# Two LayerNorms of an encoder block: three of eight quarter turnings go by DMA, one weight tile's low half moves, and the matmuls behind them go by pairs of K tiles

## The chip, the cores and the metric

One core of a Trainium2 chip runs the whole program. The metric is the device time in microseconds (us) of one execution; several executions of each kernel are timed and their median is given. Engines: TensorE (PE; PEld is its weight load), VectorE (DVE), ScalarE (ACT), GpSimd (POOL) and SyncE (SP, whose queue issues most DMAs).

## The reference

One encoder layer on 256 tokens of width 2048, all in float32, weights read once from HBM:

```python
h = x
h = LN(alpha*h + 0.5*SwiGLU_1(h))          # ln_ffn1
h = LN(alpha*h + hybrid_mixer(h))          # ln_mix
h = LN(alpha*h + CrossAttn(h, LN(mem)))    # ln_x
h = LN(alpha*h + 0.5*SwiGLU_2(h))          # ln_ffn2
# hybrid_mixer: proj = u @ w_in, split into q, k, v of a chunked attention,
# two latents, and two gates; then both attentions, gating and w_out
def layer_norm(x, g, b):
    mu = x.mean(-1); var = square(x - mu).mean(-1)
    return (x - mu) * rsqrt(var + eps) * g + b
```

## The kernel before

**Tiling.** The 256 tokens are two token tiles (tt 0 and 1) of 128. The width of 2048 is 16 K tiles of 128, kept as four blocks T0 to T3 of four K tiles each: the normalised activations turned, features on partitions, as a high and a low half. The residual stream stays as h0 and h1, one tile of 128x2048 for each token tile (`h0_101`, `h1_102` in the order; without numbers `h_101`, `h_102`).

**Matmuls.** A float32 product is made of three passes over halves: high x high, high x low, low x high. Of each weight tile (1 MB, `raw`, read by the SP queue at L193, three buffers in turn) ACT rounds two pieces of 1024 columns to the high half (`halves`, L264), and DVE subtracts to make the low half (L267). High and low halves of a tile lie in two buffers in turn, or, where a tag names a home, in blocks such as H5/H0 or X0/X1 that stay until both token tiles have used them. A weight tile is 128x2048: four K tiles of 512 columns, or a pair of K tiles of 2 x 512 columns.

**A LayerNorm after a projection.** `ln_scale` takes mean and scale from the statistics: an aggregation (L395) and eight small steps (L400 to L403) on DVE. `ln_T` then does one quarter (q) after the other, 512 columns each, eight quarters for both token tiles: normalise h on DVE (even q) or on ACT (odd q), four PE transposes of 128x128 into a PSUM tile `at` (L421), gain and bias on the way out, two on ACT (L428) and two on DVE (L430), and `split`: a rounding on ACT (L255) and the low half on DVE (L256), both into T0 (q = 0) to T3 (q = 3).

**A LayerNorm that turns by DMA.** The one in the middle, ln_mix, uses `turned_norm`: ACT copies a normalised quarter into two planes of 16-bit words (`planes`, L846), the SP queue sends a DMA transpose of 128x1024 words (`send`, L850), ACT joins the two planes again (`join`, L854), and gain and bias (L1426 on ACT, L1428 on DVE) and the split follow.

**The stretch behind ln_ffn1 and ln_x.** Four weight tiles are used twice, first with token tile 0, then with token tile 1 (`skewed`), so that PE has work on tile 0 while tile 1 is still being normalised. After ffn1 these are the value weights w_va (`val` in `mixer`): one column half n = 0 with four K tiles for each weight tile, 48 matmuls for tile 0, 48 for tile 1; then column half n = 1 with both tiles, 96 matmuls. After the cross attention, `first_group` does the same with the first gate columns of ffn2 and then its first up columns. Behind them come w_gate groups and ffn2 groups, which go by `pair_group` and `mm_pair`: a pair of K tiles, two column groups and both token tiles, four PSUM tiles at once, and form sums of activations and of weights for some pairs (`Sums`, `forms_step`).

**Order.** The program is written as a list of steps with the weight tiles they need (`add`); `weave` puts side steps, the LayerNorm's among them, between main steps, and `run` emits weight loads and halves some tiles ahead. The tile framework keeps each engine's order by this list and by priorities; `issue_after` puts an instruction behind another in the order without a semaphore of its own. Each queue, SP's too, goes in its order: an instruction that waits holds what is behind it. A load in `fetch` stands behind the last transpose sent (`self.sent`), and `send` stands behind the last load.

## Time and profile before

| what | us |
|---|---|
| median of 3 executions | 2433.03 (2432.76 to 2437.99) |
| the profiled execution | 2432.52 |
| its span on the core | 2430.7 |
| PE busy in the span | 2422.3 |
| DVE busy | 2130.9 |
| ACT busy | 1553.2 |
| matmuls and transposes on PE | 11280 instructions |

How to read it: the span runs from the first to the last instruction of one profiled execution; its own time lies 1.8 us above it. "Busy" of PE is modelled, and a matmul that stands and waits for its operand can count as busy, so small waits show only when times between two rows are held against the number of matmuls between them. The chain of waits follows the last instruction back to what released it; where it names PE, PE was the engine on which the end depended.

### The profile page before, as it was taken

To read this page: it belongs to the slowest core of one execution; us is meant where nothing else is said; L and a number is where in the kernel's file an instruction comes from. 1 tells how busy PE (TensorE), PEld (TensorE's weight loads), DVE (VectorE), ACT (ScalarE), POOL (GpSimd) and SP (SyncE) were. 2 spreads that over 40 slices of the span, in tenths; PEclk is the share of its full clock that TensorE was granted. 3 is DMA by queue.
4 is the path that set the end of the run, shared out by engine and by line. 5 is a ranking of instruction groups with operands and counts; after the bars stand their busy time and mean duration, and the time that the engine had idled before them with its cause. 6 is when DMAs were issued, how large, how long until landed. Compare 5 with 4: busy or idle time off the path is not lost.

```text
span 2430.7 us, 29702 instructions
## 1 busy us (share of the span) xinstructions
PE 2422.3 (100%) x11280; PEld 2022.8 (83%) x11280; DVE 2130.9 (88%) x2437; ACT 1553.2 (64%) x2022; POOL 35.9 (1%) x81
## 2 busy tenths in 40 slices
PE   9999999999999999999999999999999999999999
PEld 8888888888888888888888888888888888888887
DVE  8999989899889998779788889979879999888997
ACT  6676745666555557878565687765666675556662
POOL 0000000000000001000000000000000000000000
PEclk9999999999999999999999999999999999999999
DMA  7766656667656657776577577655556766666665
GB/s 268 252 212 214 207 200 222 210 201 219 224 176 215 216 195 248 229 210 176 183 246 256 167 241 213 220 181 192 190 199 214 229 221 210 220 207 207 200 220 182
DMA packets 176414, 516.20 MB, mean 212 GB/s; under 512 B 111728, under 2 KB 112496, under 8 KB 121104
## 3 DMA queue, kind: packets, MB, share of 16 engines
q1 hardware_dynamic: 170816, 495.83, 61.6%
q0 software_dynamic: 4592, 17.30, 2.2%
q8 instruction: 88, 1.44, 0.2%
q10 hardware_dynamic: 864, 1.18, 0.1%
q14 instruction: 54, 0.44, 0.1%
HBM read 485.30 MB, written 2.10 MB: 201 GB/s over the span
## 4 chain that ended last, share of the span: by engine, by line
PE 89%; DVE 4%; ACT 3%; DMA 1%; issue 1%; SPq 0%; DVEq 0%; ACTq 0%
PE at L311 24%; PE mm L311 23%; PE at L366 11%; PE mm L366 11%; PE mm L298 10%; PE mm L277 4%; PE mm L279 2%; DVE lo L267 2%; ACT hi L264 1%; PE at L1034 1%; PE at L1505 0%; PE at L277 0%; DMA raw<-w_xv 0%; PE at L1088 0%; ACT H L854 0%
## 5 line engine op out<-in xcount | busy, mean ns | idle before, releaser
L264 ACT CAST hi<-raw 128x1024 fp32r<-128x1024 f32 (+1 forms) x852 | 804.0, 981 | 458.0 <-PE at L311 150.1
L267 DVE TENSOR_TENSOR lo<-raw,hi 128x2048 fp32r<-128x2048 f32 (+1 forms) x427 | 902.0, 2114 | 134.8 <-ACT hi L264 129.0
L311 PE MATMUL mm<-hi,T 128*128 128x512 f32 (+1 forms) x1312 | 307.5, 384 | 0.8 <-DVE v L400 0.7
L311 PEld LDWEIGHTS mm<-hi,T 128*128 128x128 f32 x1312 | 244.5, 188 | 46.9 <-DVE v L400 1.1
L264 ACT CAST X<-H 128x1024 fp32r<-128x1024 f32 (+1 forms) x170 | 174.8, 1035 | 160.9 <-DVE H L248 119.9
L311 PE MATMUL at<-hi,T 128*128 128x512 f32 x1136 | 272.3, 390 | 0.0
L311 PEld LDWEIGHTS at<-hi,T 128*128 128x128 f32 x1136 | 213.3, 188 | 44.5
L267 DVE TENSOR_TENSOR X<-H,X 128x2048 fp32r<-128x2048 f32 (+1 forms) x85 | 191.4, 2252 | 64.7 <-ACT X L264 64.7
L311 PE MATMUL mm<-lo,T 128*128 128x512 f32 (+1 forms) x656 | 158.4, 383 | 0.0
L311 PE MATMUL at<-lo,T 128*128 128x512 f32 x568 | 141.0, 389 | 0.0
L311 PEld LDWEIGHTS mm<-lo,T 128*128 128x128 f32 x656 | 122.3, 188 | 22.4
L311 PE MATMUL at<-hi,H 128*128 128x512 f32 x560 | 133.8, 390 | 0.0
L311 PEld LDWEIGHTS at<-lo,T 128*128 128x128 f32 x568 | 106.7, 188 | 22.1
L311 PEld LDWEIGHTS at<-hi,H 128*128 128x128 f32 x560 | 105.0, 188 | 21.5
L250 DVE TENSOR_TENSOR H<-H,raw 128x512 f32<-128x512 f32 (+1 forms) x170 | 115.4, 679 | 2.2
L311 PE MATMUL mm<-hi,H 128*128 128x512 f32 x480 | 115.5, 392 | 0.1
L311 PEld LDWEIGHTS mm<-hi,H 128*128 128x128 f32 x480 | 89.6, 188 | 18.9 <-DVE w L684 0.5
L248 DVE TENSOR_TENSOR H<-raw 128x1024 f32<-128x1024 f32 (+1 forms) x85 | 102.1, 1201 | 0.6 <-DMA raw<-w_gate 0.4
L366 PE MATMUL mm<-X,X 128*128 128x512 f32 x342 | 91.4, 393 | 0.0
L264 ACT CAST X<-raw 128x1024 fp32r<-128x1024 f32 (+1 forms) x54 | 55.4, 1035 | 47.9 <-DVE raw L250 38.6
L366 PE MATMUL at<-X,X 128*128 128x512 f32 (+1 forms) x315 | 82.6, 386 | 0.7 <-ACT X L264 0.7
L854 ACT COPY w<-w 128x1024 uint16<-128x1024 uint16 (+1 forms) x60 | 75.7, 1275 | 1.4 <-DMA w<-w 1.4
(387 smaller groups left out, 4151.3 us busy)
## 6 DMA issues: line engine op xcount, KB each, us to landing
raw<-ffn_w_in SPq DMA_DIRECT2D x150, 1024.0 KB, 4.9
raw<-ffn_w_out SPq DMA_DIRECT2D x66, 1024.0 KB, 4.9
raw<-w_gate SPq DMA_DIRECT2D x32, 1024.0 KB, 4.8
raw<-ffn_w_out_r SPq DMA_DIRECT2D x16, 1024.0 KB, 4.9
raw<-w_qk SPq DMA_DIRECT2D x16, 1024.0 KB, 5.6
raw<-w_o_b SPq DMA_DIRECT2D x16, 1024.0 KB, 4.8
raw<-w_out SPq DMA_DIRECT2D x16, 1024.0 KB, 5.0
raw<-w_xk SPq DMA_DIRECT2D x16, 1024.0 KB, 5.4
```

Source lines behind the costliest of these rows:

```text
L248: self.nc.vector.tensor_tensor(two[0], two[1], raw[:, :m].unsqueeze(1).to_broadcast([P, 2, m]), ALU.add)
L250: self.nc.vector.tensor_tensor(t[:, a * m:a * m + m], t[:, b * m:b * m + m], raw[:, a * m:a * m + m], ALU.add)
L264: self.last_hi = self.nc.scalar.copy(hi[:, c:d], src[:, c:d])
L267: self.last_lo = self.nc.vector.tensor_tensor(lo[:, :n], src, hi[:, :n].bitcast(F32), ALU.subtract)
L277: self.nc.tensor.matmul(ps, hi[j], x.both(kt), start=(j == 0), stop=False)
L279: self.last_mm = self.nc.tensor.matmul(ps[:, :S], lo[j], x.at(0, kt), start=False, stop=(j == n - 1))
L298: self.last_mm = self.nc.tensor.matmul(ps, x.at(xi, kt)[:, tt * P:(tt + 1) * P], w[wi][:, j * 512 + c:j * 512 + c + m], start=(start and j ...
L311: self.last_mm = self.nc.tensor.matmul(ps[tt, g][:, :n], x.at(xi, kt)[:, tt * P:(tt + 1) * P], w[wi][:, c:c + n], start=first and j + wi + ...
L366: self.last_mm = self.nc.tensor.matmul(bank[:, :m], a[xi], v[wi][:, c * m:(c + 1) * m], start=own and first and wi + xi == 0, stop=own and ...
L854: self.nc.scalar.copy(self.words(u, n).rearrange("p (c k) -> p k c", k=2), self.words(s, n).rearrange("p (k c) -> p k c", k=2))
L1034: nc.tensor.matmul(ps[:, c0:c0 + nk], q[:, tt * P:(tt + 1) * P], k[:, :nk], start=(j == 0), stop=(j == len(parts) - 1))
```

## The change

It touches the LayerNorm behind ffn1 and the one behind the cross attention in the same way, and the stretch of matmuls behind each.

- Of eight quarters three go by planes, DMA transpose and join: q = 2 and q = 3 of token tile 0 and q = 3 of token tile 1. The planes and joined data lie in the blocks F and X2. Five quarters stay on PE: 20 transposes instead of 32.
- The low half of the third weight tile (H0 after ffn1, X1 after the cross attention; tag "after") is put behind the last low half of token tile 0's quarters, where it stood ahead of them.
- The planes are put behind the rounding of T1, the transposes between weight loads, the joins behind roundings of weight tiles.
- The weights are packed by pairs of K tiles, and `skewed_pairs` takes the place of `val` and of `first_group`'s own steps: token tile 0 with K tiles 0 to 7 and both column groups (48 matmuls), token tile 1 with the same (48), then K tiles 8 to 15 with both token tiles (96). The value copies come after all of these. The form sums move from between the second column half's steps to steps 9 and on.
- Two groups behind, w_gate and w_lat, take the other of two PSUM banks.

```diff
@@ run(), load() @@
         for i in range(len(main) + 1):
             for f in side.get(i, ()):
-                self.add(f, prio=prio, held=main[i][2] if i < len(main) else 0)
+                f, p = f if isinstance(f, tuple) else (f, prio)
+                self.add(f, prio=p, held=main[i][2] if i < len(main) else 0)
...
                 with self.tc.issue_after(first.ins) if first else nullcontext():
-                    got = self.halves(raw[:, :ap.shape[1]], hi, lo)
+                    got = self.halves(raw[:, :ap.shape[1]], hi, lo, bool(tags) and "after" in tags)
@@ split(), halves() @@
-        self.nc.vector.tensor_tensor(lo, src, hi.bitcast(F32), ALU.subtract)
+        self.last_split = self.nc.vector.tensor_tensor(lo, src, hi.bitcast(F32), ALU.subtract)
         return copied
-    def halves(self, src, hi, lo):
+    def halves(self, src, hi, lo, late=False):
...
-        with self.tc.issue_after(self.chain.ins) if self.chain is not None else nullcontext():
-            self.last_lo = self.nc.vector.tensor_tensor(lo[:, :n], src, hi[:, :n].bitcast(F32), ALU.subtract)
+        def low(behind=None):
+            first = behind or self.chain
+            with self.tc.issue_after(first.ins) if first is not None else nullcontext():
+                self.last_lo = self.nc.vector.tensor_tensor(lo[:, :n], src, hi[:, :n].bitcast(F32), ALU.subtract)
+        if late:
+            self.late.append(low)
+        else:
+            low()
@@ ln_T() @@
             turned = self.split(v, hi, lo)
-            if q == 1:
-                self.ln_act = turned
+            if q == qs[-1]:
+                self.ln_act, self.ln_lo = turned, self.last_split
+        while self.late:
+            self.late.pop(0)(self.ln_lo)
@@ first_group() @@
-        first = self.collect(lambda: self.skewed(
-            part, (), (None, None, ("X0", "X1", "early"), ("H4", "H5"))))
-        self.weave(first, dict(zip((0, 3, 4), before)))
...
+        side = dict(before)
+        for i, c in enumerate(SUMS_IN):
+            side.setdefault(9 + i, []).append((self.forms_step(fx, SUMS_IN, c, xT), 0))
+        self.skewed_pairs(self.t[tag + "_w_in"][0], ps, xT, side, (None, None, ("X0", "X1", "early", "after"), ("H4", "H5")))
@@ new @@
+    def skewed_pairs(self, src, ps, xT, side, tags):
+        kept = {}
+        def add(k, tts, tags=None, held=0, keep=False, again=False):
+            def fn(w=None):
+                if keep:
+                    kept[k] = w
+                w = kept.pop(k) if again else w
+                if k == 0:
+                    ps.update({(tt, g): self.group_tile(0) for tt in tts for g in range(2)})
+                self.mm_pair(ps, w, 512, xT(), (2 * k, 2 * k + 1), k == 0, k == 7, tts)
+            self.add(fn, *(() if again else ((src[:, k * 2048:(k + 1) * 2048], tags),)), held=held)
+        def build():
+            self.skewed(lambda tt, k, **kw: add(k, (tt,), **kw), (), tags)
+            for k in range(4, 8):
+                add(k, (0, 1))
+        self.weave(self.collect(build), side)
@@ mixer() @@
-        self.weave(first, {0: a, 3: b, 4: c})
...
-        second = self.collect(lambda: [val(1, (0, 1), g, ps1) for g in range(4)])
...
+        side = dict(steps(1))
+        for i, c in enumerate(SUMS_GATE):
+            side.setdefault(9 + i, []).append((self.forms_step(fx, SUMS_GATE, c, xT), 0))
+        side[12].insert(0, values)
+        self.skewed_pairs(t["w_va"][0], ps, xT, side, (None, None, ("H5", "H0", "early", "after"), ("X0", "X1", "turned")))
@@ turned_norm() @@
-    def turned_norm(self, ln, st, x):
+    def turned_norm(self, ln, st, x, homes=("X2", "X3", "H5", "H4")):
...
+        def near(tt, qs=(0, 1)):
+            def fn():
+                if tt == 0:
+                    x["T"] = self.act(["T0", "T1", "T2", "T3"])
+                self.ln_T(self.h[tt], got[tt], tt, ln, x["T"], qs)
+            return fn
...
-                nc.vector.tensor_scalar(hs, hs, mean, r, ALU.subtract, ALU.mult)
-                with self.tc.issue_after(self.next_hi.ins):
+                with nullcontext() if homes[0] else self.tc.issue_after(self.ln_lo.ins):
+                    nc.vector.tensor_scalar(hs, hs, mean, r, ALU.subtract, ALU.mult)
+                with self.tc.issue_after((self.next_hi if homes[0] else self.ln_act).ins):
                     self.planes(hs, e[q][:, tt, 0, :], 512)
...
+        if not homes[0]:
+            def low(f, *a):
+                return f(*a), 0
+            side = {0: [scale(1)], 1: [low(planes, 0, 2), low(planes, 0, 3)], 2: [low(send, 0, 2)],
+                    3: [low(send, 0, 3), near(1)], 5: [near(1, (2,)), low(planes, 1, 3)],
+                    6: [low(join, 0, 2), low(send, 1, 3)], 7: [low(join, 0, 3)], 9: [low(join, 1, 3)]}
+            return lambda tt: side if tt else ([scale(0)], [near(0)], [])
@@ build() @@
-        ln = [self.ln_steps(n, st, x) for n in ("ln_ffn1", "ln_mix", "ln_x")]
+        ln = [self.turned_norm("ln_ffn1", st, x, (None, None, "F", "X2")), None, self.turned_norm("ln_x", st, x, (None, None, "F", "X2"))]
@@ host packing @@
-    r["ffn2_gate"] = _tok(a["ffn2_w_in"][0][:, :512])
-    r["ffn2_up"] = _tok(a["ffn2_w_in"][0][:, D_FF:D_FF + 512])
...
-    r["w_va"] = _tok(w[:, 2 * aw:3 * aw])
+    r["w_va"] = _pairs(*_halves(w[:, 2 * aw:3 * aw]), 512, [()])
```

The order of PE behind ffn1, before, from the first transposes on (at: the PSUM tile of a quarter; h_101 is token tile 0, h_102 token tile 1; mm_5015 is ffn1's last output, mm_5229 the first value tile):

```order
L421 MATMUL at_5145<-ident,h_101 128x128 x4
L421 MATMUL at_5158<-ident,h_101 128x128 x4
L298 MATMUL mm_5015<-X_750_4968,H_707_4680 128x512 x6
L298 MATMUL mm_5015<-X_751_4969,H_707_4680 128x512 x3
L421 MATMUL at_5182<-ident,h_101 128x128 x4
L421 MATMUL at_5195<-ident,h_101 128x128 x4
L298 MATMUL mm_5229<-hi_4997,T_768_5140 128x512 x8
L298 MATMUL mm_5229<-lo_4998,T_768_5140 128x512 x4
L298 MATMUL mm_5229<-hi_5030,T_769_5141 128x512 x8
L298 MATMUL mm_5229<-lo_5031,T_769_5141 128x512 x4
```

and now (mm_5203 and mm_5204 are the two column halves of token tile 0):

```order
L429 MATMUL at_5144<-ident,h_101 128x128 x4
L429 MATMUL at_5157<-ident,h_101 128x128 x4
L306 MATMUL mm_5015<-X_750_4968,H_707_4680 128x512 x6
L306 MATMUL mm_5015<-X_751_4969,H_707_4680 128x512 x3
L319 MATMUL mm_5203<-hi_4997,T_768_5139 128x512
L319 MATMUL mm_5204<-hi_4997,T_768_5139 128x512
L319 MATMUL mm_5203<-hi_4997,T_768_5139 128x512
L319 MATMUL mm_5204<-hi_4997,T_768_5139 128x512
L319 MATMUL mm_5203<-hi_4997,T_768_5139 128x512 x2
L319 MATMUL mm_5204<-hi_4997,T_768_5139 128x512 x2
```

The second pair of quarters is gone from between ffn1's last matmuls and the first matmul on T0, and the first two weight tiles both work on T0. Now, at the transposes of token tile 1:

```order
L319 MATMUL mm_5203<-H_762_5050,T_769_5140 128x512
L319 MATMUL mm_5204<-H_762_5050,T_769_5140 128x512
L319 MATMUL mm_5203<-H_762_5050,T_769_5140 128x512
L319 MATMUL mm_5204<-H_762_5050,T_769_5140 128x512
L429 MATMUL at_5250<-ident,h_102 128x128 x4
L429 MATMUL at_5263<-ident,h_102 128x128 x4
L319 MATMUL mm_5203<-X_782_5198,T_769_5140 128x512 x2
L319 MATMUL mm_5204<-X_782_5198,T_769_5140 128x512 x2
L319 MATMUL mm_5203<-X_782_5198,T_769_5140 128x512 x2
```

The four matmuls ahead of the transposes are the first use of the third weight tile's low half (H_762); they use T1 of token tile 0, where they used T2 before.

The order of DVE at the end of token tile 0's quarters, before (w: gain and bias out of PSUM; H_762 stood ahead of this piece, before the aggregation of token tile 0):

```order
L256 TENSOR_TENSOR T_768_5140<-w_773_5150,T_768_5140 128x4x128
L754 TENSOR_TENSOR h_102<-h_102,mm_5015 128x512
L256 TENSOR_TENSOR T_769_5141<-w_775_5163,T_769_5141 128x4x128
L390 BN_STATS bn_4815<-h_102 128x6
L430 TENSOR_SCALAR w_777_5187<-at_5182,vecs 128x128
L395 BN_AGGR mv_5207<-bn_4815 128x2
L430 TENSOR_SCALAR w_779_5200<-at_5195,vecs 128x128
L400 TENSOR_SCALAR v_5208<-mv_5207 128x1
```

and now:

```order
L258 TENSOR_TENSOR T_768_5139<-w_773_5149,T_768_5139 128x4x128
L725 TENSOR_TENSOR h_102<-h_102,mm_5015 128x512
L258 TENSOR_TENSOR T_769_5140<-w_775_5162,T_769_5140 128x4x128
L398 BN_STATS bn_4815<-h_102 128x6
L271 TENSOR_TENSOR H_762_5050<-raw_5047,H_761_5049 128x2048
L403 BN_AGGR mv_5181<-bn_4815 128x2
L1387 TENSOR_SCALAR h_101<-h_101,mv_5088,y_5090 128x512
L408 TENSOR_SCALAR v_5182<-mv_5181 128x1
L1387 TENSOR_SCALAR h_101<-h_101,mv_5088,y_5090 128x512
```

The low half H_762 (128x2048) lies between the statistics and the aggregation of token tile 1, and two normalisations of h_101 stand among the steps of that aggregation in place of the gain and bias of two quarters.

The order of SP, loads of w_va, before:

```order
L193 DMA raw_5047<-w_va 128x2048
L193 DMA raw_5222<-w_va 128x2048
L193 DMA raw_5345<-w_va 128x2048
L193 DMA raw_5364<-w_va 128x2048
L193 DMA raw_5422<-w_va 128x2048
L193 DMA raw_5463<-w_va 128x2048
```

and now (raw_5301 is the fifth of eight loads; F and X are the blocks of planes):

```order
L195 DMA raw_5047<-w_va 128x2048
L195 DMA raw_5196<-w_va 128x2048
L841 DMA_TRANSPOSE F_5217<-F_5217 128x8x128
L841 DMA_TRANSPOSE X_787_5220<-X_787_5220 128x8x128
L195 DMA raw_5301<-w_va 128x2048
L195 DMA raw_5335<-w_va 128x2048
L841 DMA_TRANSPOSE X_787_5220<-X_787_5220 128x8x128
L195 DMA raw_5405<-w_va 128x2048
L195 DMA raw_5453<-w_va 128x2048
```

Two transposes stand ahead of the fifth load and one ahead of the seventh.

## Rows read from the trace of the kernel before

**Rows 1.** The page, part 1: engines, busy time, share of the span, instructions.
```profile
PE 2422.3 (100%) x11280; PEld 2022.8 (83%) x11280; DVE 2130.9 (88%) x2437; ACT 1553.2 (64%) x2022; POOL 35.9 (1%) x81
```

**Rows 2.** Chain of waits, 610 to 760 us: start, length, what.
```profile
680.29 1.04 PE at L421 x8
...
683.41 0.87 PE at L421 x8
...
697.20 32.66 PE mm L298 x144
729.85 5.44 PE mm L311 x24
```

**Rows 3.** Chain of waits, 1690 to 1830 us.
```profile
1737.85 0.87 PE at L421 x8
...
1787.70 10.88 PE at L311 x48
```

**Rows 4.** Windows: busy of PE, PEld, DVE, ACT, POOL, granted clock, DMA share, GB/s.
```profile
680.00:690.00 10.00, 10.00 (x52) 8.15 (x51) 8.32 (x24) 8.34 (x16) 0.00 (x0) 1.00 0.18 72
690.00:700.00 10.00, 10.00 (x54) 8.42 (x52) 9.17 (x20) 7.52 (x15) 0.00 (x0) 1.00 0.30 105
...
710.00:720.00 10.00, 10.00 (x46) 8.29 (x45) 5.79 (x14) 5.17 (x8) 0.00 (x0) 1.00 0.61 207
```

**Rows 5.** Tile X, 1380 to 1425 us: xcount, ns min/median/max, first and last start.
```profile
L1426 ACT ACTIVATE X<-X,vecs x8: 480/504/517, 1389.7 to 1412.9; 128x128 f32<-128x128 f32 x8
...
L846 ACT COPY X<-h x4: 1038/1044/1046, 1383.9 to 1390.7; 128x1024 uint16<-128x1024 uint16 x4
L850 SPq DMA_TRANSPOSE X<-X x4: 1231/1232/3229, 1385.0 to 1391.9; - x4
L854 ACT COPY X<-X x4: 1361/1368/1384, 1388.3 to 1407.6; 128x1024 uint16<-128x1024 uint16 x4
...
DMA to landing us min/median/max: 3.0/4.6/7.6
```

**Rows 6.** Timeline of ACT, 676 to 700 us: start, length, instruction, [idle before <-releaser].
```profile
693.16 1.83 ACT L428 ACTIVATE w<-at,vecs 128x128 f32<-128x128 f32 x4 [1.00 <-PE at L421]
```

**Rows 7.** Timeline of DVE, 676 to 700 us.
```profile
675.01 2.27 DVE L267 TENSOR_TENSOR H<-raw,H 128x2048 fp32r<-128x2048 f32 x1
677.20 0.26 DVE L395 BATCH_NORM_AGGREGATE mv<-bn 128x2 f32<-128x24 f32 x1
...
679.55 0.16 DVE L403 SCALAR_TENSOR_TENSOR nb<-mv,y 128x1 f32<-128x1 f32 x1
...
683.68 0.69 DVE L256 TENSOR_TENSOR T<-w,T 128x512 fp32r<-128x512 f32 x1 [0.34 <-ACT T L255]
684.29 0.68 DVE L754 TENSOR_TENSOR h<-h,mm 128x512 f32<-128x512 f32 x1
...
691.43 2.29 DVE L267 TENSOR_TENSOR X<-raw,X 128x2048 fp32r<-128x2048 f32 x1
693.65 1.79 DVE L430 TENSOR_SCALAR w<-at,vecs 128x128 f32<-128x128 f32 x4
695.68 1.29 DVE L256 TENSOR_TENSOR T<-w,T 128x512 fp32r<-128x512 f32 x2 [0.24 <-ACT T L255]
```

**Rows 8.** Timeline of DVE, 1736 to 1758 us.
```profile
1740.86 1.29 DVE L256 TENSOR_TENSOR T<-w,T 128x512 fp32r<-128x512 f32 x2 [0.26 <-ACT T L255]
...
1753.54 1.29 DVE L256 TENSOR_TENSOR T<-w,T 128x512 fp32r<-128x512 f32 x2 [0.25 <-ACT T L255]
```

**Rows 9.** The page, part 5: group of instructions, busy, mean ns, idle before.
```profile
L264 ACT CAST hi<-raw 128x1024 fp32r<-128x1024 f32 (+1 forms) x852 | 804.0, 981 | 458.0 <-PE at L311 150.1
```

**Rows 10.** The page's DMA issues, all queues: xcount, KB each, median us to landing.
```profile
raw<-w_va SPq DMA_DIRECT2D x8, 1024.0 KB, 5.7
```

**Rows 11.** Line 850, the DMA transposes: xcount, ns min/median/max; the landing of all.
```profile
L850 SPq DMA_TRANSPOSE H<-H x12: 1231/1238/7732, 1250.0 to 1418.3; - x12
...
DMA to landing us min/median/max: 2.7/3.2/12.9
```

More of the change, by code (lines that the diff above doesn't have):

```diff
@@ L122, in __init__ @@
         self.cut = self.early = False
+        self.late = []
     def name(self, s):
@@ L301, in mm_tok, with mm_pair @@
                     )
-    def mm_pair(self, ps, w, n, x, kts, first, last):
+    def mm_pair(self, ps, w, n, x, kts, first, last, tts=(0, 1)):
         for wi in range(2):
             for j, kt in enumerate(kts):
-                for tt in range(2):
+                for tt in tts:
                     for g in range(2):
@@ L873, in mixer, with values @@
         e = self.__dict__
-        va, kept, ps1 = {}, {}, {}
-        def val(n, tts, g, ps, tags=None, held=0, keep=False, again=False):
-            def fn(w=None):
-                if keep:
-                    kept[g] = w
-                w = kept.pop(g) if again else w
-                for tt in tts:
-                    if g == 0:
-                        ps[tt] = self.mm_tile()
-                    self.mm_tok(ps[tt], tt, w, xT(), range(4 * g, 4 * g + 4), g == 0, g == 3)
-                if g == 3:
-                    if "t" not in va:
-                        va["t"] = self.block("H4", (P, 2, 1024))
-                    for tt in tts:
-                        (nc.vector.tensor_copy if tt else nc.scalar.copy)(
-                            va["t"][:, tt, n * 512:(n + 1) * 512], ps[tt])
-            ap = t["w_va"][n, :, g * 2048:(g + 1) * 2048]
-            self.add(fn, *(() if again else ((ap, tags),)), held=held)
-        ps = {}
-        first = self.collect(lambda: self.skewed(
-            lambda tt, g, **kw: val(0, (tt,), g, ps, **kw), (),
-            (None, None, ("H5", "H0", "early"), ("X0", "X1", "turned"))))
-        a, b, c = steps(1)
-        self.weave(first, {0: a, 3: b, 4: c})
-        gates, fx = {}, {}
-        second = self.collect(lambda: [val(1, (0, 1), g, ps1) for g in range(4)])
-        self.weave(second, {1 + i: [self.forms_step(fx, SUMS_GATE, c, xT)] for i, c in enumerate(SUMS_GATE)}, prio=0)
+        va, ps, gates, fx = {}, {}, {}, {}
+        def values():
+            va["t"] = self.block("H4", (P, 2, 1024))
+            for n in range(2):
+                for tt in range(2):
+                    (nc.vector.tensor_copy if tt else nc.scalar.copy)(
+                        va["t"][:, tt, n * 512:(n + 1) * 512], ps[tt, n])
+        side = dict(steps(1))
[3 more added lines that the diff above has]
+        self.skewed_pairs(t["w_va"][0], ps, xT, side, (None, None, ("H5", "H0", "early", "after"), ("X0", "X1", "turned")))
         bias = {}
@@ L1393, in fn @@
             def fn():
[L1394 removed]
+                if tt == 0 and homes[0]:
                     x["T"] = self.act(["T0", "T1", "T2", "T3"])
```

47 lines of the change are left out of this document (6 added, 41 removed).

## The prediction

> **What bounds the kernel now.** I read the page first, then the chain of waits, then the timelines of the two stretches that the change touches. The page says that TensorE (PE) is busy for 2422.3 of 2430.7 us [rows 1]: only work taken off PE, or a stall taken off it, can shorten the kernel, and anything that makes PE stand still lengthens it. The chain shows where PE's time goes in the two LayerNorms: matmuls of 128x512 one behind the other at 32.66 / 144 = 0.2268 us each, and packets of eight PE transposes of 0.87 us (0.109 each) [rows 2, 3]. The windows give a granted clock of 1.00 there and 10.00 us of busy PE in each 10 us [rows 4], so the clock plays no part. PE counts as busy while a matmul waits for its operand, so small waits must be found by subtraction. After ffn1: from 680.29 to 729.85, where the first w_gate group begins, 49.56 us pass [rows 2]; the 201 matmuls and 32 transposes in it need 201 x 0.2268 + 32 x 0.109 = 49.07, so 0.5 us is waiting. After the cross attention: 1737.85 to 1787.70 is 49.85 [rows 3], against 204 matmuls and 32 transposes, 49.75: 0.1 us. So there is next to no wait to be removed, and the gain can come only from PE's transposes.
>
> **What is removed.** Three of eight quarter turnings per LayerNorm leave PE: 12 transposes x 0.109 = 1.31 us, 2.61 us for both. The order shows the same number of matmuls before and after. With the 0.6 us of old waits the best case is 3.2 us off. That the matmuls go by pairs of K tiles, with two PSUM tiles in turn, costs nothing: the same 0.2268 per matmul stands in the w_gate groups, which have that form already (5.44 for 24) [rows 2].
>
> **What is added, off PE.** Each quarter turned by DMA costs ACT a copy into planes (1.04), a joining copy (1.37) and two scalings (0.50 each), the SP queue a transpose (1.23 to issue, 3.0 to 7.6 to land, median 4.6), and DVE two scalings [rows 5]; the splitting stays. The rows are those of the LayerNorm in the middle of the kernel, which turns its tiles this way already. What goes is the copies out of PSUM, two on ACT (1.83 for four) [rows 6] and two on DVE. So ACT gains about 2.5 us of work per quarter, 7.5 per LayerNorm, DVE nothing. ACT works 5.17 to 8.34 us of each 10 here [rows 4]: there is room on average; what counts is the order.
>
> **Where PE can wait, in its own order.**
>
> (a) *First matmuls of token tile 0.* Before, eight transposes (0.87) stood between the last ffn1 matmuls and the first matmul on T0, and T0's low half had that long to be made. Now PE arrives 0.87 earlier. The low half begins at 683.68 [rows 7]; PE would want it at 683.41 + 0.45. ACT no longer normalises a second quarter just ahead, so it may begin 0.4 earlier. Bounds 0 to 0.5 us after ffn1; after the cross attention 0 to 0.2.
>
> (b) *First matmuls of token tile 1.* This is the tightest place. On DVE, in order, stand: low half of T0, add to h1, low half of T1, statistics (0.60 from start to start each [rows 7]); the moved low half of a weight tile (2.19: 675.01 to 677.20); the chain from the aggregation to the scale (677.20 to 679.55, 2.35) with two normalisations of h0 between its steps (0.7 to 0.9 more, since part falls into gaps); the normalisations of h1 (0.91); another weight tile's low half (2.22: 691.43 to 693.65); scalings, rounding and low half of T0 (2.5, from 693.65 and 695.68, a little less because ACT's part is done ahead). That is 13.4 us. From 683.3 it ends at 696.7; before, the same low half ended at 696.37 [rows 7]. After the cross attention the same sum from 1740.86 ends at 1754.3, before at 1754.19 (half of the pair at 1753.54) [rows 8]. So the moved low half, which left the chain of tile 0 where PE did not wait for it, now lies in the chain of tile 1 and takes back what was saved: PE, arriving about 0.9 us sooner than before in each LayerNorm, waits about 0.9 to 1.4 us. Its cover was the work that DVE did there before on the quarters now turned by DMA.
>
> From that point PE still has 142 matmuls and four transposes, 32.2 + 0.44 = 32.6 us: 729.3 and 1786.9, before further waits.
>
> (c) *K tiles 8 to 11 of token tile 0 (block T2).* They come through the DMA path and stand far back on ACT: two roundings of the fifth weight tile (2.0, each 0.98 [rows 9]; held until PE lets go of the first tile, 1.5 us after the point above), a scaling, the join, a scaling, two roundings of the sixth tile, scalings, a rounding, the second join, two scalings, the planes of the third quarter, then T2's rounding: 11 to 11.9 us, so ready 12.5 to 13.4 after the point. PE asks for it after 52 matmuls and four transposes, 12.2. Wait 0.2 to 1.25; I take 0.6, since ACT's instructions overlap a little at their ends in every row.
>
> So the w_gate group begins at 729.9 (before 729.85) and the ffn2 group at 1787.5 (before 1787.70). **Sum:** 2432.52 + 0.05 - 0.2 = 2432.4 against the profiled execution. The median of the runs, 2433.03, lies 0.5 above that execution, so a median of **2433.0** is expected: no change.
>
> **The SP queue.** The first two transposes stand between the fourth and the fifth weight load, the third ahead of the seventh. A transpose can't be issued before its planes, and the loads behind it wait too, also where their buffers are free. I put the planes of h0 at 690.1 to 692 (behind (b)'s normalisations), the two transposes at 691.3 and 692.5, the fifth load just behind; by 5.7 us [rows 10] it lands at about 698.3. ACT wants it at 698.2. That is no margin, and part of what (c)'s upper end stands for. The third transpose goes at about 709.9 and lands by the median at 714.5; join, scalings, rounding and low half (3.6 us) end at 718.1, and PE asks for T3 at about 719. The seventh load goes at 711.1, lands at 716.8, and is rounded by 718.8. Margins under 1 us. The DMA engines are free at 680 to 700 (shares 0.18 and 0.30 [rows 4]), so bandwidth isn't the trouble, order is.
>
> **Rivals.**
>
> *A, the forecast (0.60):* the saved transposes come back as waits at (a), (b) and (c); own range 2432.0 to 2434.2 from the bounds of (c) and (b).
>
> *B, the cover holds (0.22):* DVE reaches the second weight tile's low half sooner than I add up, ACT runs T2 early, and PE goes from matmul to matmul. Then 2433.0 - 2.6 = 2430.4, and 2429.8 if the 0.6 us of old waits goes too. For it: ACT and DVE have idle time in both stretches [rows 4], and before, h1's chain made PE wait 0.5 us at the most. Against it: the sums above, which leave no slack in DVE's order between 683 and 696.
>
> *C, slower (0.18):* a transpose lands late and what is queued behind SP or ACT goes with it. From the third transpose's issue PE needs T3 in about 9.1 us, and 3.6 of it is work after landing: it decides at a landing of about 5.5 us. At 7.6, the longest in the middle LayerNorm [rows 5], PE waits 2 us in each stretch: 2437.0. At 12.9, the longest of all transposes [rows 11], 7 us each: 2447; and an issue itself can hold SP for 3.2 to 7.7 us [rows 5, 11], which delays the weights one for one. For it: ACT waits for joins, and loads stand right around these transposes. Against it: the median is 4.6.
>
> By the rows, four turnings on PE take 0.44 us, and the same quarter by DMA 1.04 + 4.6 + 1.37 before it can be scaled [rows 2, 5]. The Trainium skill ("VectorE: DVE Perf Modes", The three transpose paths and Rules for kernel authors) says the same as a rule: turn 128x128 on TensorE where PSUM will do, else by DMA. By that rule the change loses, as in C; the rule weighs one turning alone, and here PE is the bound and the DMA path lies beside it.
>
> That the change does not do what it says is excluded by the order, which shows 20 transposes for 32 on PE in both places.
>
> **How the numbers follow.** What a measurement of this kernel can tell from no change is about 0.2%, 4.9 us: below 2428.2 or above 2437.9. A and B lie inside. Of C two thirds lie above (0.12), the rest inside. Faster gets 0.03 for effects behind the stretches, where sums and forms now come later on DVE; no row prices them. The range goes from B's best, 2429.8, to C at a landing of 7.6, 2437.0: it leaves out the far part of C and the 0.03.
>
> **What would show it.** In the chain of the changed kernel: 20 transposes in each stretch, 729 to 730.5 at the first w_gate group and 1787 to 1788.5 at the ffn2 group. In the timeline: no transposes between ffn1's last matmuls and T0's first; T0's low half for tile 1 ending near 696.7 and 1754.3; T2's rounding for tile 0 near 709 to 710; the third transpose's landing. B shows itself by a w_gate group at 728.1 to 728.6. The forecast is wrong if PE stands at the fifth weight tile or at T3 for over 1.5 us, or if DVE, with its later sums, holds up the w_gate groups.

## The result and the profile after

The changed kernel takes **2441.54 us** in the median of 9 runs (2440.03 to 2443.89), the kernel before 2435.26 (9 runs, 2432.62 to 2439.24). The ratio is 1.0028 with the 95% interval 1.0019 to 1.0037: **slower** by about 6.8 us by the ratio (the two medians lie 6.3 apart), where no change (2433.0) was forecast and 2437.0 was the upper end. The profiled execution took 2441.54, its span 2439.8, at a granted clock of 1.00.

Part 1 of the page after, which answers to [rows 1]:

```profile
PE 2424.0 (99%) x11256; PEld 2017.6 (83%) x11256; DVE 2132.9 (87%) x2441; ACT 1563.8 (64%) x2030; POOL 36.0 (1%) x81
```

24 transposes are gone, and PE's busy time is longer all the same: a matmul that waits for an operand counts as busy. So the time has to be found between rows of the chain. From ffn1's transposes to the ffn2 group (start, length, what):

```profile
680.10 0.45 PE at L429 x4
...
708.61 9.32 DMA X<-X
...
718.01 1.35 ACT X L845
...
724.14 2.30 DVE lo L271
...
734.03 5.44 PE at L319 x24
...
818.85 10.88 PE at L319 x48
...
1336.26 43.55 PE at L319 x192
...
1443.99 6.03 DMA raw<-w_xq
...
1706.15 40.80 PE mm L306 x180
...
1762.87 3.28 PE mm L319 x12
...
1796.89 10.88 PE at L319 x48
```

Before, the chain through the stretch behind ffn1 was PE from end to end; now it leaves PE behind the first transposes, at 680.55, and again at 698.29, and its longest piece up to the w_gate group is the third DMA transpose. The same rows of before stand at 680.29, 729.85 and 1787.70 [rows 2, 3], and, for the three not shown ahead, in the chain of before at:

```profile
812.33 10.88 PE mm L311 x48
...
1330.12 43.55 PE at L311 x192
...
1697.04 40.80 PE mm L298 x180
```

The two spans differ by 9.1 us, the last rows above by 1796.89 - 1787.70 = 9.19. Piece by piece, after less before: from the transposes to the first w_gate group 53.93 - 49.56 = **+4.37**; on to the row of 48 matmuls, 84.82 - 82.48 = **+2.34**; 517.41 - 517.79 = -0.38; from the row of 192 to that of 180 matmuls 369.89 - 366.92 = **+2.97**; from there to the ffn2 group 90.74 - 90.66 = +0.08; with -0.19 up to the first transposes, 9.19. So the second LayerNorm came out level, as forecast, and three places lost time: PE at T3 after ffn1, the w_gate groups, and the stretch of the cross attention. The profiled execution of before lies 2.7 us under the median of its nine, and some of the +2.97 is its own spread (below).

**The third transpose.** Timelines of after: PE (the wait, and what ended it), ACT (the join), SP.

```profile
717.02 1.97 PE L319 MATMUL mm<-lo,T 128*128 128x512 f32 x8
722.36 3.92 PE L319 MATMUL mm<-hi,T 128*128 128x512 f32 x16 [3.37 <-ACT hi L266]
726.48 2.11 PE L319 MATMUL mm<-lo,T 128*128 128x512 f32 x8 [0.20 <-DVE lo L271]
```

```profile
718.01 1.34 ACT L845 COPY X<-X 128x1024 uint16<-128x1024 uint16 x1 [7.86 <-DMA X<-X]
```

```profile
708.61 1.23 SPq L841 DMA_TRANSPOSE X<-X  x1
709.93 1.12 SPq L195 DMA_DIRECT2D raw<-w_va  x2
711.18 28.63 SPq L195 DMA_DIRECT2D raw<-w_gate  x5
```

PE stands for 3.37 us, then 0.20, and its 16 matmuls take 3.92 where 16 x 0.2268 is 3.63: 3.9 us in all. The high half that it waits for is the seventh weight tile's, which ACT rounds behind the join. ACT idles 7.86 us in front of the join; the transpose landed 9.32 us after its issue. What else moved? A queue to which the prediction had not turned, POOL's; first after, then before:

```profile
708.14 1.23 POOL L886 DMA_DIRECT2D X<-gate_row  x2 [705.88 <-PE mm L319]
```

```profile
708.72 1.23 POOL L912 DMA_DIRECT2D X<-gate_row  x2 [706.46 <-ACT w L255]
```

Two loads of the gates' bias row, spread over 128 partitions, go out as soon as block X1 is free; they did so before, too, when nothing waited for a transfer there. Now they start 0.5 us ahead of the transpose. The DMA view of after from 708.6 to 718.0 (queue, kind: packets, MB, share of 16 engines; then issues with the us to landing):

```profile
q1 hardware_dynamic: 1104, 0.66, 48.9%
q0 software_dynamic: 288, 1.05, 45.9%
q8 instruction: 1, 0.02, 0.7%
...
raw<-w_va SPq DMA_DIRECT2D x2, 1024.0 KB, 11.4
X<-gate_row POOLq DMA_DIRECT2D x2, 512.0 KB, 6.7
...
X<-X SPq DMA_TRANSPOSE x1, 9.3
```

and from 1775.5 to 1779.0, the third transpose of the other LayerNorm, where POOL loads nothing:

```profile
q1 hardware_dynamic: 1076, 0.43, 65.8%
...
X<-X SPq DMA_TRANSPOSE x1, 3.1
```

The same transpose takes 3.1 us alone and 9.3 beside POOL's queue (q0), whose packets took 45.9% of the engines' 9.4 us, 4.3 us of each. The Trainium skill ("DMA: Bandwidth & Descriptors", Queues, rings and completion order) says that each DMA engine takes turns between the queues that have work, packet by packet; the trace fits that, with 1104 packets of SP's queue and 288 of POOL's in this window, though it doesn't show the single turns. As an estimate, 3.1 + 4.3 = 7.4 of the 9.3 us are so accounted for. One packet more lies in this window, 16 KB of instructions (q8). In e5 below such a packet falls into the same transpose without any load of POOL, and it lands after 4.5 us: that would be 1.4 us of the other 1.9, and 0.5 stays open.

### The profile page after: what moved, and what is told of

The parts are those of the page before. It is cut to its first block, busy times and chain, and to the rows that moved or that the text cites. A ratio compares the mean times of both kernels' runs of the same rounds, so it can differ in the third digit from the quotient of the medians.

```text
span 2439.8 us, 29679 instructions
## 1 busy us (share of the span) xinstructions
PE 2424.0 (99%) x11256; PEld 2017.6 (83%) x11256; DVE 2132.9 (87%) x2441; ACT 1563.8 (64%) x2030; POOL 36.0 (1%) x81
## 2 busy tenths in 40 slices
DMA packets 182753, 517.79 MB, mean 212 GB/s; under 512 B 118065, under 2 KB 118833, under 8 KB 127441
## 4 chain that ended last, share of the span: by engine, by line
PE 90%; DVE 5%; ACT 3%; DMA 1%; issue 1%; DVEq 0%; ACTq 0%; SPq 0%
PE at L319 26%; PE mm L319 25%; PE mm L374 11%; PE at L374 11%; PE mm L306 7%; PE mm L285 5%; PE mm L287 2%; DVE lo L271 1%; ACT hi L266 1%; PE at L1008 1%; DMA raw<-w_xq 1%; PE at L1494 0%; PE at L1062 0%; PE at L285 0%; DMA X<-X 0%
## 5 line engine op out<-in xcount | busy, mean ns | idle before, releaser
L319 PE MATMUL mm<-hi,T 128*128 128x512 f32 (+1 forms) x1424 | 337.5, 385 | 5.0 <-ACT hi L266 3.4
L319 PEld LDWEIGHTS mm<-hi,T 128*128 128x128 f32 x1424 | 264.6, 188 | 59.4 <-ACT hi L266 3.8
L319 PE MATMUL at<-hi,T 128*128 128x512 f32 x1216 | 291.2, 389 | 0.0
L319 PEld LDWEIGHTS at<-hi,T 128*128 128x128 f32 x1216 | 228.2, 188 | 47.7
L319 PE MATMUL mm<-lo,T 128*128 128x512 f32 (+1 forms) x712 | 173.6, 383 | 0.2 <-DVE lo L271 0.2
L319 PEld LDWEIGHTS mm<-lo,T 128*128 128x128 f32 x712 | 132.6, 188 | 25.3 <-DVE lo L271 0.6
L319 PE MATMUL at<-lo,T 128*128 128x512 f32 x608 | 150.3, 389 | 0.0
L319 PEld LDWEIGHTS at<-lo,T 128*128 128x128 f32 x608 | 114.1, 188 | 23.7
L250 DVE TENSOR_TENSOR H<-raw 128x1024 f32<-128x1024 f32 (+1 forms) x85 | 102.0, 1200 | 2.6 <-DMA raw<-ffn_w_in 1.6
L374 PE MATMUL mm<-X,X 128*128 128x512 f32 x360 | 96.3, 392 | 0.0
L374 PEld LDWEIGHTS mm<-X,X 128*128 128x128 f32 x360 | 66.7, 188 | 16.3 <-DVE X L271 2.6
```

What stands on the lines that cost most here:

```text
L250: self.nc.vector.tensor_tensor(two[0], two[1], raw[:, :m].unsqueeze(1).to_broadcast([P, 2, m]), ALU.add)
L319: self.last_mm = self.nc.tensor.matmul(ps[tt, g][:, :n], x.at(xi, kt)[:, tt * P:(tt + 1) * P], w[wi][:, c:c + n], start=first and j + wi + ...
L374: self.last_mm = self.nc.tensor.matmul(bank[:, :m], a[xi], v[wi][:, c * m:(c + 1) * m], start=own and first and wi + xi == 0, stop=own and ...
```

## The experiments

**Theory:** the bias loads on POOL's queue make the third transpose late, and that, with what queues behind it, is the loss. **Rivals:** the moved low half; the third turning by DMA as such, with the seventh weight load behind it on SP; the place of the join on ACT. All kernels stand in one table, all from the chain's rows as above ("third landing": us from issue to landing of the third DMA transpose after ffn1; "to gate": transposes to first w_gate group; "gates": on to the 48 matmuls; "cross": the 192 to the 180 matmuls; "LN2": on to the ffn2 group; us). The ratios are to executions of before timed beside each kernel (medians 2433.97 to 2435.26). With * the first w_gate matmul is read from PE's timeline, as the chain has no row there; that puts it some 0.17 us early, so "to gate" is so much too short and "gates" too long. What PE waits for late in "to gate" it need not wait for in "gates", so the two are read together.

| kernel | median us | ratio (95%) | third landing | to gate | gates | cross | LN2 |
|---|---|---|---|---|---|---|---|
| before | 2435.26 | 1 | - | 49.56 | 82.48 | 366.92 | 90.66 |
| e8, before again | 2434.01 | 1.0000 (0.9990 to 1.0010) | - | 49.57 | 82.40 | 368.43 | 90.66 |
| e11, before again | 2431.87, one execution | - | - | 49.14 | 82.41 | 367.30 | 90.66 |
| changed | 2441.54 | 1.0028 (1.0019 to 1.0037) | 9.3 | 53.93 | 84.82 | 369.89 | 90.74 |
| e1 | 2440.61 | 1.0026 (1.0015 to 1.0036) | 8.0 | 52.44* | 85.05 | 368.89 | 90.72 |
| e2 | 2443.07 | 1.0035 (1.0022 to 1.0049) | 9.7 | 56.23 | 82.81 | 368.72 | 91.08 |
| e3 | 2440.70 | 1.0024 (1.0014 to 1.0034) | 9.6 | 55.81 | 82.54 | 369.88 | 90.11 |
| e4 | 2436.78 | 1.0009 (1.0000 to 1.0018) | none | 50.56 | 82.53 | 369.25 | 91.57 |
| e5 | 2437.63 | 1.0017 (1.0009 to 1.0026) | 4.5 | 49.79 | 84.25 | 369.55 | 90.77 |
| e6 | 2436.64 | 1.0011 (1.0002 to 1.0020) | 4.7 | 48.82* | 84.71 | 369.62 | 90.08 |
| e7 | 2438.54 | 1.0017 (1.0007 to 1.0026) | 11.0 | 55.01 | 82.47 | 369.90 | 90.74 |
| e9 | 2434.62 | 0.9998 (0.9989 to 1.0007) | 4.6 | 49.22 | 82.44 | 370.88 | 90.10 |
| e10 | 2434.72 | 1.0003 (0.9994 to 1.0012) | 4.4 | 49.06 | 82.52 | 369.59 | 90.14 |
| e12 | 2435.00 | 1.0002 (0.9993 to 1.0011) | 4.7 | 49.04 | 82.49 | 369.90 | 90.13 |
| e13 | 2442.60, one execution | - | 9.6 | 56.25* | 82.79 | 370.19 | 90.79 |

**The clock in these rows.** In the profiles of e2, e3, e7 and e13 the granted clock fell from 1.00 to 0.50 (1.2 for 2.4 GHz) while PE stood at the third transpose after ffn1, for 3.0 to 3.8 us, or just behind that wait, and was back 3 to 7 us later; in the profile of the changed kernel, with a wait of 3.37 us, it stayed at 1.00. Here e3, one window (the clock is the third figure from the end) and PE's row:

```profile
723.00:724.00 1.00, 1.00 (x4) 0.81 (x3) 1.00 (x3) 0.90 (x3) 0.00 (x0) 0.50 0.96 401
```

```profile
721.90 6.70 PE L319 MATMUL mm<-hi,T 128*128 128x512 f32 x16 [3.64 <-ACT hi L266]
```

The 16 matmuls that take 3.92 us in the changed kernel's profile take 6.70 here and 6.32 in e2; in e7 11 matmuls take 1.5 us more than at full clock. So 1.5 to 2.8 us of "to gate" in these four are the clock's, and "gates" gives most of it back: both together are 139.04 (e2), 138.35 (e3), 137.48 (e7) and 139.04 (e13) for 138.75. Of the nine executions of the changed kernel eight have a mean clock of 0.998 or 0.999 and the profiled one 1.000; where it fell in those eight no trace shows.

**e1, the bias loads earlier.**

```diff
+                bias["t"] = self.block("H3", (P, 2, 1024))
+            if n == 2:
+                bias["u"] = self.block("X1", (P, 2, 1024))
...
+        self.add(lambda: [load_bias(n) for n in range(2)])
         self.skewed_pairs(t["w_va"][0], ps, xT, side, (None, None, ("H5", "H0", "early", "after"), ("X0", "X1", "turned")))
...
-        self.add(lambda: [load_bias(n) for n in range(2)])
```

> The two gate_row loads on POOL's queue, which the changed kernel issues 0.5 us ahead of the third transpose after ffn1, go to block H3 instead and are issued some 28 us sooner; nothing else moves on any engine. Theory (the third transpose shares the DMA engines with these loads): it lands after 3.0 to 4.6 us instead of 9.3, the first w_gate group starts at 729 to 730.3 instead of 734.0, and the whole is 4 to 6 us shorter than the changed kernel, 2435.5 to 2437.5. Rival (the transpose is late for another reason, the weight loads of its own queue or its planes): it lands after about 9 us again and the whole stays at 2441.5.

It did not test this. POOL's timeline:

```profile
680.86 1.24 POOL L887 DMA_DIRECT2D H<-gate_row  x2 [678.59 <-PE at L429]
708.26 1.05 POOL L887 DMA_DIRECT2D X<-gate_row  x2 [26.16 <-PE mm L319]
```

The first two loads went early, and the next two, which had come far later, took their place at the moment block X1 fell free: landing 8.0 us. A miss, but it shows that the block's release, not the program's text, sets the moment.

**e2, two loads beside the other LayerNorm's third transpose.**

```diff
+        def extra():
+            b = self.block("H4", (P, 2, 1024))
+            for n in range(2):
+                self.nc.gpsimd.dma_start(b[:, n, :], self.t["gate_row"][n:n + 1, :].to_broadcast([P, 1024]))
+        side.setdefault(8, []).append(extra)
```

> The changed kernel with two more loads of 512 KB on POOL's queue behind the cross attention, into a block that is just free, so that they are issued within 2 us of the third transpose there, as gate_row is after ffn1; nothing reads them. Theory (collision with POOL's loads): the third transpose lands after 7 to 10 us instead of 3.1 to 3.3, the second ffn2 group starts 3 to 5 us later than 1796.9, and the whole is about 2445. Rival (the loads do no harm): 3.3 us again and 2441.5.

The DMA view of e2, 1775 to 1782:

```profile
H<-gate_row POOLq DMA_DIRECT2D x2, 512.0 KB, 5.0
X<-X SPq DMA_TRANSPOSE x1, 5.8
```

The loads went out 1.1 us ahead of the transpose, and its landing went from 3.1 to 5.8 us: POOL's packets delay it here too, though less than the 7 to 10 us that were expected. The stretch lost 0.34 us only, not 3 to 5. A landing of about 5.5 is what the prediction named as the point from which PE waits, so 5.8 costs little, as it should.

**e3, the moved low half put back in both places.**

```diff
-        self.skewed_pairs(t["w_va"][0], ps, xT, side, (None, None, ("H5", "H0", "early", "after"), ("X0", "X1", "turned")))
+        self.skewed_pairs(t["w_va"][0], ps, xT, side, (None, None, ("H5", "H0", "early"), ("X0", "X1", "turned")))
```

> The changed kernel with the moved low half of the third weight tile back ahead of token tile 0's aggregation, in both stretches; otherwise the order stays. Theory (b) of the prediction, that this low half lies in token tile 1's chain and PE waits for it: tile 1's first low half of T0 ends 1.5 to 2.2 us sooner, PE's wait there of about 1 us goes in each stretch, the whole is 1 to 2 us shorter than the changed kernel. Rival (the wait at tile 1 is set by ACT or by PE itself): no change. Second rival (tile 0's chain was helped by the move): PE waits at the first transposes and the whole gets 1 to 3 us longer.

Where nothing else is in the way, behind the cross attention, it saves 90.74 - 90.11 = 0.63 us. After ffn1 the late transpose (9.6) and the lower clock hide it: 55.81 + 82.54 = 138.35 against 138.75 in the changed kernel. So the low half is a true cost of the change, and a small one. The chain of e3 is PE again, with eight transposes in one packet where after has its chain on ACT and DVE:

```profile
1750.36 8.38 PE mm L319 x36
1758.74 0.87 PE at L429 x8
1759.61 5.71 PE mm L319 x24
```

**e4, two quarters by DMA instead of three** (token tile 1's q = 3 is turned on PE).

```diff
-                    5: [near(1, (2,)), low(planes, 1, 3)],
-                    6: [low(join, 0, 2), low(send, 1, 3)], 7: [low(join, 0, 3)], 9: [low(join, 1, 3)]}
+                    5: [near(1, (2, 3))], 6: [low(join, 0, 2)], 7: [low(join, 0, 3)]}
```

> Only two quarters of token tile 0 go by DMA; the third, of tile 1, goes back to PE's transposes, in both stretches. Theory (the loss lies in the third transpose after ffn1): the w_gate group starts at 729.7 to 730.7, PE has 0.44 us more to do in each stretch, the whole is 3 to 5 us shorter than the changed kernel, 2436.5 to 2438.5. Rival (the loss lies in the pairs of K tiles and in the later sums): the w_gate group is early, but the w_gate groups lose as much behind it, and the whole stays within 1.5 us of 2441.5.

The wait at T3 goes (50.56 for 53.93), and so does the loss in the w_gate groups: of 6.7 us after ffn1 all but 1.1 is back. But "LN2" grows by 0.83: where nothing collides, the third turning by DMA is worth having there.

**e5, the later pair of bias loads gated.** As e1, and each of the later two loads waits for a copy on POOL (128x1, one element of each partition) from the product that it will be added to.

```diff
+            if n > 1:
+                nc.gpsimd.tensor_copy(bias["u"][:, n % 2, :1], gates[n - 2][:, 1, 0, :1])
```

> As e1, but now no load of POOL's queue is left near the third transpose: rows 0 and 1 of gate_row go to H3 at about 681 us, rows 2 and 3 are held by a copy of one element on POOL until the gate product before is made. (In e1 the second pair, no longer held by a product, took the first pair's place at 708.3 us.) Theory (collision): the third transpose after ffn1 lands after 3.0 to 4.6 us, the w_gate group starts at 729.3 to 730.4, the whole is 4 to 6.5 us shorter than the changed kernel: 2435 to 2437.5. Rival (late for another reason): 8 to 9.7 us and 2440 to 2442 again.

The DMA view from 709.1 to 714.0 shows no POOL queue, and:

```profile
q8 instruction: 1, 0.02, 1.2%
...
X<-X SPq DMA_TRANSPOSE x1, 4.5
```

"To gate" falls from 53.93 to 49.79. **This settles the first loss:** the same order on PE, ACT, DVE and SP in this stretch, POOL's loads out of the way, and 4.1 of 4.37 us are back. The w_gate groups still lose 1.8, and the median, 2437.63, lies just above the range expected. The landing is 4.5 and not 3.1: in e5, e6, e9, e10 and e12 the 16 KB packet of instructions falls about 2 us into this transpose, which lands after 4.4 to 4.7 us, while the quarters that are turned by DMA with neither such a packet nor a load of POOL beside them land after 3.0 to 3.3 in both stretches of every profile. No run moves the packet alone.

**e6, e5 with the low half back.**

> e5 and e3 together: no POOL load near the transpose, and the low half of the third tile back in token tile 0's chain. If the two causes add up: both stretches lose PE's wait at token tile 1, the first is 0.6 to 1.2 us shorter than in e5, the second 0.5 to 0.7 us shorter than before, and the whole 0.5 to 2 us below e5: 2433.5 to 2436, level with the kernel before or just below it. Rival (with the transposes on time PE is held by something else there, T2 or the weights): no difference to e5.

"To gate" 48.82, "LN2" 90.08: each below before, by some 0.6 and 0.58. The median, 2436.64, is above the 2433.5 to 2436 expected. "Gates" stays at 84.71, and its chain says why:

```profile
718.86 2.28 DVE lo L271
...
721.17 4.88 DMA raw<-w_gate
...
726.08 0.07 DVE H L250
```

The low half of the seventh value tile frees a weight buffer; a w_gate load into it takes 4.88 us; the first sum of w_gate weights (L250) waits for that. Before, this sum began at 722.39 with no wait; in the changed kernel at 731.35, waiting for the load.

**e7, the seventh weight load put ahead of the third transpose on SP, the join one step later; the bias loads where they were.**

```diff
+            if not isinstance(w, Sums) and any(w[0] is p for p in self.pre):
+                fetch(i + 1)
...
+            if k == 5:
+                self.pre.append(ap)
...
-                    6: [low(join, 0, 2), low(send, 1, 3)], 7: [low(join, 0, 3)], 9: [low(join, 1, 3)]}
+                    6: [low(join, 0, 2), low(send, 1, 3)], 7: [low(join, 0, 3)], 10: [low(join, 1, 3)]}
```

> The gate_row loads stay where the changed kernel has them; instead the seventh weight load goes ahead of the third transpose in SP's order, and the join behind that tile's roundings on ACT. Theory (what costs most is not the late turning itself but the weight tile queued behind it, on SP's queue, where it landed after 11.4 us): the transpose lands late again, but the seventh tile is rounded by about 712, PE waits only for T3 of token tile 1 at about 721.5 instead of for the tile's low half at 726.5, and the w_gate group starts 3 to 5 us sooner, 729.5 to 731. Rival (PE waits for the turning): the w_gate group stays at 733 to 735. Order and time of some sums behind it change too.

```profile
708.45 10.98 DMA X<-X
...
722.77 0.70 DVE T L260
...
723.52 11.44 PE mm L321 x43
734.96 5.44 PE at L321 x24
```

PE now waits for the turning itself (landing 11.0), no longer for a weight, and "to gate" is no better: 55.01, or 53.5 without the clock's 1.5. The group starts at 734.96, as the rival had it: the load's place alone is not what cost the 4.37. "Gates" is 82.47 and the first w_gate sum, at 727.64, waits for no load; but since PE reaches these groups late here, this alone would prove little.

**e9, all three: e6 and the seventh load ahead.**

> e6 with the seventh weight load ahead of the third transpose in SP's order. In e5 and e6 the first w_gate groups lose 1.8 to 2.1 us that e4 (no third transpose) does not lose: DVE and ACT come late to the sums of the first w_gate weights. Theory (the weight loads stand behind the third transpose on SP's queue until 709 us, so roundings, low halves and sums come late): with one load ahead of it, the first w_gate groups lose under 0.8 us, and the whole is 1.2 to 2.2 us below e6, 2434 to 2435.5, level with the kernel before. Rival (the sums are late because joins, scalings and T3's halves stand in DVE's and ACT's order): the loss of 1.8 to 2.1 stays.

```profile
729.50 5.44 PE at L321 x24
...
1760.31 30.29 PE mm L321 x132
1790.60 10.88 PE at L321 x48
```

The first w_gate sum begins at 723.73 instead of 726.08 and waits for no load, and "to gate" and "gates" together fall from 133.53 to 131.66. **This shows where the second loss lies:** in the weight buffer that the seventh tile frees late. Its low half begins at 716.18 instead of 718.86, and the w_gate load into that buffer goes at 718.50 instead of 721.17. Why the tile is late, the run doesn't separate. The edit moves the load alone, but the order on ACT and DVE moves with it; first e6, then e9, ACT's join and the tile's two roundings (timelines from 703 to 728):

```profile
712.71 1.35 ACT L845 COPY X<-X 128x1024 uint16<-128x1024 uint16 x1 [3.25 <-DMA X<-X]
...
715.98 1.99 ACT L266 CAST hi<-raw 128x1024 fp32r<-128x1024 f32 x2
```

```profile
712.94 1.36 ACT L850 COPY X<-X 128x1024 uint16<-128x1024 uint16 x1 [3.17 <-DMA X<-X]
714.15 2.00 ACT L268 CAST hi<-raw 128x1024 fp32r<-128x1024 f32 x2
```

In e6 the seventh load, issued at 709.25, had landed after 5.9 us, at 715.1, and ACT rounded it only behind the join, its scalings and two other roundings; in e9 the roundings stand right behind the join. Estimated from these rows, the load's landing accounts for at most 1.0 of the 2.7 us by which the low half comes sooner, and the order on ACT and DVE for the rest.

Both stretches are now at or under before: 49.22 + 82.44, and "LN2" 90.10. In time e9 is level with before: 0.9998 (0.9989 to 1.0007), some 7 us better than the change as made. Both stretches together gain 0.5 to 0.9 us against before's three executions (131.55 to 132.04, 90.66), and "cross" takes it back. **e10** moves the join behind those roundings as well, with no gain; since they already stand ahead of the scalings in e9, it doesn't test the order that e6 had:

> e9 with the third quarter's join behind the seventh tile's roundings on ACT. If ACT's order matters once the transpose lands in time (3 to 5 us), the seventh tile's halves are ready sooner and T3 of token tile 1 up to 2 us later; PE asks for both at the same place. Theory: no gain over e9, within 0.7 us in both stretches. Rival (ACT's wait at the join holds roundings): 0.5 to 1.5 us shorter.

**The cross attention.** Its order is the same on every engine, yet "cross" is 366.9 to 368.4 in the three executions of before, and 368.7 to 370.9 in every one with the change or a part of it. **e8** and **e11** are before itself:

> The kernel before, unchanged, for a second profile. In all five profiles with the change, the stretch from the w_gate groups to the LayerNorm after the cross attention is 2.3 to 4.9 us longer than in the one profile of before, 2 to 3 of it around the w_xq loads, where neither order differs. Theory (that part is spread between executions: before has runs from 2432.3 to 2439.6): the second profile differs from the first by 1 to 6 us there and by under 0.3 in the two stretches of the change. Rival (the change costs it): the second profile agrees with the first within 0.5 us.

> The kernel before, unchanged, a third profile: how far the stretch around the w_xq and w_xk loads spreads between executions of one kernel. The second profile had 1.4 us more there than the first, the eight with the change 1.7 to 3.0 us more. If the part is spread, the third lies between 0 and 3 us over the first; if 1 us or more of it belongs to the change, the three of before stay under 1.5 us.

Is it that the new packing puts the weights elsewhere in memory? **e12** (e9) and **e13** (the changed kernel) keep the two dropped arrays in the list of inputs, unread:

```diff
+    r["ffn2_gate"] = _tok(a["ffn2_w_in"][0][:, :512])
+    r["ffn2_up"] = _tok(a["ffn2_w_in"][0][:, D_FF:D_FF + 512])
```

> e9 with two inputs that no instruction reads: the packed weights of the first ffn2 group, which the kernel before has as inputs of their own and the change dropped, at the same place in the list of inputs. In ten profiles with the change the stretch from the long matmul run at about 1336 us to the LayerNorm after the cross attention takes 368.7 to 370.9 us, in the three of before 366.9 to 368.4, with the same order on every engine. Theory (where the weights lie in memory decides how fast that stretch's loads land, and two dropped inputs moved them): 366.9 to 368.4 us again, and the whole 1 to 2.5 us below e9, 2432.5 to 2434. Rival (spread, or something else of the change): 368.7 to 370.9 again and 2434.6.

> The changed kernel itself with the same two unread inputs, a second sample of the same question: 366.9 to 368.4 us for the stretch around the cross attention if the place of the weights in memory decides, 368.7 to 370.9 if not. The stretch behind ffn1 stays as in the changed kernel, the third transpose landing after 9 to 11 us.

e12: 369.90. e13, one execution: 2442.6 us, landing 9.55, "cross" 370.19. As far as the list of inputs sets the place, the place is not it. Before alone spreads by 1.5 us, but none of the twelve profiles with the change lies inside that spread: the means are 367.6 and 369.7, 2.1 apart. One part can be read. In the chain after, a w_xq load stands at 1443.99 with 6.03 us (above), in before's there is none at this place. In the three of before this load lands within 4.7 to 4.8 us, in all twelve with the change after 5.7 to 6.3. The DMA view of the changed kernel from 1443.9 to 1450.1 has a row that before's has not in the same place:

```profile
q8 instruction: 1, 0.02, 1.0%
```

A 16 KB packet of instructions falls into this load, 1.0 to 2.9 us behind its issue in all twelve; in before's it lies ahead of it, in all three. From this load's issue to that of the second one behind it 10.1 to 10.7 us pass instead of 9.3, 0.8 to 1.4 more of the 2.1. It is the same packet size that goes with 1.4 us on the third transpose in e5. With 24 transposes fewer and other instructions, the instruction fetch may stand elsewhere against the loads; that is argued from the traces, no run isolates it, and the rest stays open.

## Why the prediction was wrong

- **(a), (b), (c): right in the main.** Of the 53.93 us after ffn1, 201 matmuls and 20 transposes need 47.8. By the starts of PE's rows the other 6.2 are 0.7 at (a), where 0 to 0.5 was forecast, 1.1 at (b) (0.9 to 1.4), 0.3 at (c) (0.2 to 1.25, 0.6 taken) and 4.1 at T3, for which the sum has no term. At (b) token tile 1's T0 low half was to end at 696.7 and ended at 695.87 + 0.69 = 696.56. T2's rounding, forecast for 709 to 710, began at 708.49. Behind the cross attention the sum was -0.2 and came out at +0.08. DVE's row and PE's at (b):

```profile
695.87 1.29 DVE L258 TENSOR_TENSOR T<-w,T 128x512 fp32r<-128x512 f32 x2 [0.33 <-ACT T L257]
```

```profile
695.89 2.38 PE L319 MATMUL mm<-hi,T 128*128 128x512 f32 x8 [0.45 <-ACT T L257]
```

- **The step that failed: "The third transpose goes at about 709.9 and lands by the median at 714.5", and "bandwidth isn't the trouble, order is".** It went at 708.61 and landed at 717.93, after 9.32 us in place of 4.6, because two loads of POOL's queue were in flight (e5 took them away: 4.5), and PE stood 3.9 us where the sum had no wait. The shares 0.18 and 0.30 were read for 680 to 700; the row of the window in which this transpose falls, 710 to 720, stood in the same group with 0.61 [rows 4], and POOL's queue, which held the cause in before's trace at 708.72, was not looked at.
- **Rival C: its price was right, its chance was not.** "It decides at a landing of about 5.5": 9.32 - 5.5 = 3.8, measured 3.9; e2 at 5.8 lost 0.34 and e5 at 4.5 almost nothing. But C took the landing from other transposes' spread and so doubled it over two stretches; it is one neighbour in one stretch. The rule of the Trainium skill that is cited there ("VectorE: DVE Perf Modes", Rules for kernel authors), TensorE for 128x128, has the sign of the result, but not for its reason: e9, e10 and e12 keep the DMA turning and are level with before. They gain nothing by it either.
- **Missing from the sum: "if DVE, with its later sums, holds up the w_gate groups"** was named as a sign, without a price: 2.34 us. What held them was a weight load, into a buffer freed late, and not the amount of DVE's work.
- **Missed: "faster gets 0.03 for effects behind the stretches".** An effect of some 2 us lay behind, on the slow side.
- What should have been gained, 2.61 us of transposes, did leave PE; but the stretch behind ffn1 grew by 4.37 + 2.34 = 6.71 all the same.

## What to carry to other kernels

Before a transfer is put on the path of PE, list what every queue, POOL's too, has in flight at that moment, and read the DMA share of that window, not of its neighbours. Loads that go out "when a block falls free" move with the change; gate them by a product that is needed later anyway. A weight tile that is rounded late costs twice: once itself, and once through the buffer that it frees late; so look at its place on ACT and DVE as well as at its load. And when PE stands for some us, look at the granted clock behind the wait before its matmuls are compared.

## Not expected of the hardware

- A transpose of 128x1024 words lands 3.0 to 3.3 us after its issue alone, 4.4 to 4.7 with a 16 KB packet of instructions in its flight, 5.8 beside two 512 KB loads issued 1.1 us earlier, and 8.0 to 11.0 beside two issued 0.5 us earlier, with such a packet as well.
- A stretch with the same order on every engine changed by some 2 us; a 16 KB instruction packet inside a 1 MB load goes with a landing of 5.7 to 6.3 instead of 4.7 to 4.8 us.
- A wait of PE of 3.0 to 3.8 us went with a fall of the granted clock from 1.00 to 0.50 in four profiles, and a wait of 3.37 with none in a fifth.
- In e5 a copy of one element for each partition (128x1) on POOL took 8.36 us the first time and 1.69 the second, by a profile that is rough on POOL.
